# Three feed-forward units at the start of an encoder kernel loaded by blocks of rows, and transposes moved a tick later

## The chip, the cores and the metric

The kernel runs on one core of one Trainium2 chip. The metric is the device time of one execution in microseconds. The engines are TensorE (PE in the profile; its weight loads are PEld), VectorE (DVE), ScalarE (ACT), GpSimd (POOL) and SyncE (SP), which issues most of the loads.

## The reference, cut to what matters

A trunk of two layers over 256 tokens of width 1024. Each layer is a SwiGLU feed-forward, a mixer with three branches, and a second SwiGLU feed-forward:

```
for l in range(2):
    x = x + 0.5 * swiglu(rms_norm(x, g1), w1, w3, w2)         # w1, w3: 1024 x 2816, w2: 2816 x 1024
    h = rms_norm(x, gm);  z = h @ w_in                        # 1024 x 6752, cut into the three branches' inputs and the gates
    y_na  = neighborhood_attention(q, k, v, rpb)
    y_gla = rms_norm(gla_bidirectional(...)) * silu(gr)       # gated linear attention
    y_mla = mla_attention(...)
    x = x + sum_i(sigmoid(gate_i) * (y_i @ w_br_i)) @ w_out
    x = x + 0.5 * swiglu(rms_norm(x, g2), w1', w3', w2')
swiglu(h, w1, w3, w2) = (silu(h @ w1) * (h @ w3)) @ w2
```

All data are float32. Three products of split numbers (hi x hi, hi x lo, lo x hi) stand for one float32 product.

## The kernel before

Weights come in units of 1 MB (128 x 2048 float32) in the order of their use. SP loads a unit into a `raw` tile (three of them); ScalarE copies it to its high part (L142) and VectorE subtracts to get the low part (L148), two halves each, into an `hl` tile (four of them). TensorE multiplies high and low parts with those of the transposed activations `xT`. `unit()` sees to it that a unit and the first half of the next are split; `fill()` splits further ahead.

The order of all instructions is the order in which the Python code issues them; each engine executes its own list in that order. Side work (drains, norms, attention steps) is written as generators. `spawn(gen, wait)` puts one on a list; each `tick()`, called after a burst of matmuls, counts the waits down and runs a generator to its next `yield n`, which sets its wait to n ticks. `finish()` runs a generator to its end at once.

PSUM has eight banks: four with the tag `acc` for bursts (`acc_t`) and four with the tag `ta` for transposes and attention products (`tr_t`, `at_t`). Buffers of a tag go round, so a new tile waits until the last reader of the tile four back has finished.

The first feed-forward has no transposes of x: `start_first` loads x already transposed (`xT` in memory) and scales it by the norm's gain (`gcol`), since the row factor can be multiplied in later. It deals with the first two w1/w3 units: unit 0 by quarters of two k-steps each, interleaved with the loads of xT, unit 1 by halves. Each unit has 8 k-steps of 128 rows; w1 and w3 are the two halves b, and each k-step and half takes three matmuls of 256 columns (`part`). Then `fform` does the 20 other units, each with 16 matmuls of 512 columns (the high weights against high and low xT at once) and 16 of 256. `rs_bcast` (its two transposes are L298) broadcasts the row factors once they are known; in the first feed-forward this stands behind the third unit, and the drains of the units before it are started there. A drain (`fdrain`) reads the accumulators (L480 on ScalarE, L481 on VectorE; L485 and L486 for the first two units), multiplies by the row factor, applies silu (L487, L489) and splits the result (L491, L493).

The feed-forward's output (`wide_out`) keeps four banks, two for each half t of the tokens, over all eleven w2 units. In the mixer the linear attention's last steps are: add its parts to `gy` (L1092), squares and row factors (L1095, L573), eight products `gy * factor * silu(gr)` (L1103), then eight transposes of `gy` (L695, by `four`), split by L246 and L247. The transposed q of the neighbourhood attention comes from `na_tr` (also L695). The branches' products are multiplied with the gates (L1181, L1184), summed (L1186), transposed by `mix_task` (L1195) and go through w_out.

## Time and profile before

| | us |
|---|---|
| median of three timed runs | 1257.64 (1256.57 to 1257.86) |
| the profiled execution, its own time | 1256.21 |
| its span in the trace | 1254.4 |
| TensorE busy | 1237.7 |
| VectorE busy | 894.8 |
| ScalarE busy | 710.4 |
| GpSimd busy | 219.4 |

The page's parts are numbered: part 1 is the busy time of each engine, part 4 the chain of work that ended last, part 5 the costliest groups of instructions. Times in the trace count from the span's start. In a timeline a run of like instructions is one row: start, length from the first start to the last end, engine, line, operation, output and inputs, shape, count, and in brackets the idle time of the engine before it with what ended it. A row can be cut by the stretch that was asked for, and its times then still are those of the whole instructions in it.

### The profile page before, as it was taken

What the parts mean: (1) busy time and instruction counts of PE and PEld (TensorE: products, weight loads), DVE (VectorE), ACT (ScalarE), POOL (GpSimd) and SP (SyncE); (2) the same over time, 40 slices, a digit from 0 to 9 for tenths busy, and PEclk for the clock granted to TensorE, in tenths of its full rate; (3) what the DMA queues carried; (4) which work ended last, traced back from release to release, by engine and by line L of the source; (5) the groups of instructions that cost most, each with busy time, mean ns of one, the idle gap of its engine ahead of it and who ended that gap; (6) DMA issues with size and microseconds to landing.
All of it is one profiled execution on the core that took longest, in us unless ns stands there. A gap on an engine that the chain in (4) does not pass through costs nothing.

```text
span 1254.4 us, 18062 instructions
## 1 busy us (share of the span) xinstructions
PE 1237.7 (99%) x6996; PEld 1058.5 (84%) x6996; DVE 894.8 (71%) x1382; ACT 710.4 (57%) x1303; POOL 219.4 (17%) x167
## 2 busy tenths in 40 slices
PE   7999999999999999999999999999999999999998
PEld 7888888889987888888888888888899878888887
DVE  5888736679755868887378886375896577788862
ACT  6556535657665465655366555355686644665541
POOL 0222101132011112221012220021322020122200
PEclk9999999999999999999999999999999999999999
DMA  8655644562543544556345556347526434555560
GB/s 304 214 185 201 234 169 160 175 222 93 197 171 132 198 172 170 200 181 248 142 171 222 184 185 241 128 162 246 175 91 208 166 134 171 199 201 174 196 235 34
DMA packets 37942, 228.58 MB, mean 182 GB/s; under 512 B 5776, under 2 KB 6928, under 8 KB 13280
## 3 DMA queue, kind: packets, MB, share of 16 engines
q1 hardware_dynamic: 37680, 227.36, 51.1%
q8 instruction: 55, 0.90, 0.3%
q14 instruction: 31, 0.25, 0.1%
q0 software_dynamic: 32, 0.07, 0.0%
q10 hardware_dynamic: 144, 0.00, 0.0%
HBM read 224.26 MB, written 1.05 MB: 180 GB/s over the span
## 4 chain that ended last, share of the span: by engine, by line
PE 93%; DVE 4%; ACT 1%; DMA 1%; issue 1%; POOL 0%; DVEq 0%; SPq 0%; ACTq 0%
PE acc L372 86%; PE ta L372 4%; DVE hl L148 2%; PE ta L695 1%; DMA raw<-in_l_f_w 1%; PE ta L263 1%; ACT junk L1095 0%; POOL sm L573 0%; PE ta L782 0%; ACT hl L142 0%; PE ta L1195 0%; PE ta L680 0%; DVE s L489 0%; DVE s L1181 0%; DVE s L1103 0%
## 5 line engine op out<-in xcount | busy, mean ns | idle before, releaser
L148 DVE TENSOR_TENSOR hl<-raw,hl 128x1024 fp32r<-128x1024 f32 (+2 forms) x422 | 568.1, 1386 | 95.4 <-ACT hl L142 84.5
L142 ACT ACTIVATE hl<-raw 128x1024 fp32r<-128x1024 f32 (+2 forms) x422 | 417.1, 1040 | 103.8 <-PE acc L372 89.9
L372 PE MATMUL acc<-xT,hl 128*128 128x512 f32 (+1 forms) x2768 | 472.8, 332 | 0.9 <-DVE s L481 0.5
L372 PEld LDWEIGHTS acc<-xT,hl 128*128 128x128 f32 x2768 | 413.6, 188 | 57.8 <-DVE s L481 0.8
L372 PE MATMUL acc<-hl,xT 128*128 128x512 f32 (+1 forms) x1584 | 361.8, 383 | 0.0
L372 PEld LDWEIGHTS acc<-hl,xT 128*128 128x128 f32 x1584 | 291.8, 188 | 46.9 <-issue 1.7
L372 PE MATMUL acc<-hl,s 128*128 128x512 f32 x1344 | 312.3, 392 | 0.9 <-DVE s L481 0.9
L372 PEld LDWEIGHTS acc<-hl,s 128*128 128x128 f32 x1344 | 252.0, 189 | 54.2 <-DVE s L481 1.3
L482 POOL TENSOR_TENSOR s<-s,rsb 128x512 f32<-128x512 f32 x80 | 111.9, 1399 | 355.8 <-DVE s L481 355.8
L491 ACT ACTIVATE s<-s 128x256 fp32r<-128x256 f32 x82 | 34.2, 418 | 172.5 <-DVE s L489 172.5
L481 DVE TENSOR_TENSOR s<-acc,s 128x256 f32<-128x256 f32 x158 | 59.7, 419 | 58.5 <-ACT s L480 58.5
L573 POOL TENSOR_TENSOR sm<-sm,mhalf 128x4 f32<-128x4 f32 (+2 forms) x24 | 35.8, 1493 | 200.4 <-DVE sm L577 198.9
L284 POOL TENSOR_TENSOR sm<-sm,mhalf 128x1 f32<-128x1 f32 x12 | 14.1, 1176 | 295.1 <-DVE sm L283 295.1
L480 ACT ACTIVATE s<-acc 128x256 f32<-128x256 f32 x158 | 50.6, 371 | 0.0
L266 ACT ACTIVATE xT<-ta,gain 128x128 fp32r<-128x128 f32 x80 | 22.8, 368 | 35.6 <-PE ta L263 35.6
L247 DVE TENSOR_TENSOR s<-ta,s 128x512 fp32r<-128x512 f32 (+1 forms) x46 | 26.7, 604 | 22.6 <-ACT s L246 22.3
L246 ACT ACTIVATE s<-ta 128x512 fp32r<-128x512 f32 (+1 forms) x46 | 23.0, 531 | 34.4 <-PE ta L695 14.7
L487 ACT ACTIVATE s<-s 128x256 f32<-128x256 f32 x82 | 34.2, 419 | 11.2 <-POOL s L482 0.8
L550 DVE SCALAR_TENSOR_TENSOR x<-acc,x 128x512 f32<-128x512 f32 (+1 forms) x20 | 11.3, 580 | 39.7 <-PE acc L372 39.7
L372 PEld LDWEIGHTS ta<-s,s 64*64 64x64 f32 (+3 forms) x720 | 30.6, 145 | 7.0 <-issue 5.9
L372 PE MATMUL ta<-s,s 64*64 64x128 f32 (+4 forms) x720 | 35.9, 260 | 0.0
L493 DVE TENSOR_TENSOR s<-s,s 128x256 fp32r<-128x256 f32 x82 | 34.0, 416 | 1.9 <-ACT s L491 1.9
(161 smaller groups left out, 643.9 us busy)
## 6 DMA issues: line engine op xcount, KB each, us to landing
raw<-in_l_f_w SPq DMA_DIRECT2D x124, 1024.0 KB, 4.8
raw<-in_l_in_g SPq DMA_DIRECT2D x16, 816.0 KB, 4.4
raw<-in_l_in_late SPq DMA_DIRECT2D x8, 1024.0 KB, 4.9
raw<-in_l_out SPq DMA_DIRECT2D x8, 1024.0 KB, 4.8
raw<-in_l_f_up SPq DMA_DIRECT2D x6, 1024.0 KB, 4.8
raw<-in_l_in_m SPq DMA_DIRECT2D x4, 1024.0 KB, 4.7
raw<-in_l_in_gr SPq DMA_DIRECT2D x4, 1024.0 KB, 4.9
raw<-in_l_in_r SPq DMA_DIRECT2D x4, 1024.0 KB, 4.8
```

Of the source, the lines that this page charges most:

```text
L142: ACT.activation(out=hls[j][:, 0, sl], in_=raws[j][:, sl], func=AF.Copy)
L148: DVE.tensor_tensor(out=hl[:, 1, sl], in0=r[:, sl], in1=hl[:, 0, sl].bitcast(F32), op=ALU.subtract)
L246: ACT.activation(out=hi, in_=ps, func=AF.Copy)
L247: DVE.tensor_tensor(out=lo, in0=ps, in1=hi.bitcast(F32), op=ALU.subtract)
L372: PE.matmul(out=out, lhsT=lhsT, rhs=rhs, start=start, stop=stop, skip_group_check=True)
L480: ACT.activation(out=g[:, j, :], in_=a[j][:, 256:], func=AF.Copy)
L481: DVE.tensor_tensor(out=g[:, j, :], in0=a[j][:, :256], in1=g[:, j, :], op=ALU.add)
L482: POOL.tensor_tensor(out=g, in0=g, in1=rb[:, None, :].to_broadcast([128, 2, 256]), op=ALU.mult)
L487: ACT.activation(out=g[:, 0, :], in_=g[:, 0, :], func=AF.Silu)
L491: ACT.activation(out=o[:, 0, :], in_=g[:, 0, :], func=AF.Copy)
L493: DVE.tensor_tensor(out=o[:, 1, :], in0=g[:, 0, :], in1=o[:, 0, :].bitcast(F32), op=ALU.subtract)
L573: POOL.tensor_tensor(out=r[:, :n], in0=ss[:, :n], in1=mhalf[:, :n], op=ALU.pow)
```

## The change

- The first three w1/w3 units, not two, go through `start_first` (FIRST_R = 3). They and xT are loaded by blocks of rows: k-step 0, k-step 1, then pairs of k-steps; for each block first xT, then that block of each of the three units (128 x 256 for one k-step, 128 x 512 for two). They land in tiles of the scratch pool (`s2`), not in `raw`.
- For each block the three units are split and multiplied one after the other. Each unit has one bank (tag `ta`), w1 in its first half and w3 in its second.
- Ahead of them TensorE does eight matmuls of 512 columns on a tile of zeros (bfloat16), which VectorE clears first.
- gcol's load is issued before ScalarE's first activation; the identity is loaded by SP behind the fourth unit, no more by POOL; x comes behind it, then the fifth and sixth units.
- `rs_bcast` stands behind the fourth unit; it is followed by that unit's drain and then those of the first three. No unit is held back any more.
- In every feed-forward `wide_out` takes the two banks of t = 1 from `ta` instead of `acc`. The mixer's `wide_out` keeps `acc`.
- In the mixer three kinds of transposes come one tick later: those of `gy` (`yield 2`), of q (`spawn(..., 4)`) and of the merged branches (`spawn(mix_task, 3)`).

```diff
-FIRST_R = 2
+FIRST_R = 3
+WARM = 8
         def start_first():
+            zero = junk(512)
+            DVE.memset(zero, 0.0)
+            ps = tr_t()
+            for _ in range(WARM):
+                PE.matmul(out=ps, lhsT=zero[:, :128], rhs=zero, start=True, stop=True, skip_group_check=True)
             POOL.memset(mhalf, -0.5)
             POOL.memset(ones, 1.0)
-            ACT.activation(out=junk(1), in_=ones, func=AF.Copy)
             nc.scalar.dma_start(out=gcol, in_=T["gcol"])
-            nc.gpsimd.dma_start(out=idt, in_=T["ident"])
-            xr = [s2((128, 2, 256)) for _ in range(4)]
...
-            for q in range(4):
-                sl = slice(q * 512, q * 512 + 512)
-                nc.sync.dma_start(out=xr[q], in_=T["xT"][:, 2 * q:2 * q + 2, :])
-                nc.sync.dma_start(out=raws[0][:, sl], in_=units[0][0][:, sl])
...
+            xr = [s2() for _ in range(4)]
+            rw = [[s2() for _ in range(4)] for _ in range(FIRST_R)]
+            groups = ((0, 1), (1, 2), (2, 4), (4, 6), (6, 8))
+            at = lambda tiles, a, b: tiles[a // 2][:, a % 2 * 256:a % 2 * 256 + (b - a) * 256]
+            for a, b in groups:
+                nc.sync.dma_start(out=at(xr, a, b), in_=T["xT"][:, a:b, :])
+                for j in range(FIRST_R):
+                    nc.sync.dma_start(out=at(rw[j], a, b), in_=units[j][0][:, a * 256:b * 256])
+            ACT.activation(out=small(1), in_=ones, func=AF.Copy)
...
+            dma_to(FIRST_R)
+            nc.sync.dma_start(out=idt, in_=T["ident"])
             for t in range(2):
                 nc.sync.dma_start(out=x[:, t, :], in_=T["x"][t * 128:(t + 1) * 128, :])
...
+            dma_to(FIRST_R + 2)
+
+            def part(acc, hl, k):
+
+                for c in range(2):
+                    o = acc[:, c * 256:c * 256 + 256].rearrange("p (t n) -> p t n", t=2)
+                    a = k * 256 + c * 128
+                    mm(o, hl[:, 0, a:a + 128], xT[:, :, 0, k, :], k == 0 and c == 0, False)
                     mm(o, hl[:, 0, a:a + 128], xT[:, :, 1, k, :], False, False)
                     mm(o, hl[:, 1, a:a + 128], xT[:, :, 0, k, :], False, k == 7)
 
-            accs = [[at_t(), at_t()], [acc_t(), acc_t()]]
...
+            accs = [at_t() for _ in range(FIRST_R)]
+            for a, b in groups:
+                sl = slice(a * 256, b * 256)
+                for k in range(a, b):
...
+                for j in range(FIRST_R):
+                    ACT.activation(out=hls[j][:, 0, sl], in_=at(rw[j], a, b), func=AF.Copy)
+                    DVE.tensor_tensor(out=hls[j][:, 1, sl], in0=at(rw[j], a, b), in1=hls[j][:, 0, sl].bitcast(F32),
+                                      op=ALU.subtract)
+                    for k in range(a, b):
+                        part(accs[j], hls[j], k)
+            st["next"] = FIRST_R
+            split_to(2 * FIRST_R + 2)
...
-        def wide_out(first, lhs, nu, done):
+        def wide_out(bank1, lhs, nu, done):
...
-                        accs[t] = (acc_t(), acc_t())
+                        accs[t] = (bank1(), bank1()) if t else (acc_t(), acc_t())
...
                 if i == (FIRST_R if first is not None else 2):
                     rs_bcast()
-                    if first is not None:
-                        for j in range(2):
-                            drains[j] = run(fdrain(j, first[j][0][:, :256], first[j][1][:, :256]))
-                        for j, a in held:
-                            drains[j] = run(fdrain(j, a))
-                if "x" in rs_b:
-                    drains[i] = run(fdrain(i, acc))
-                else:
-                    held.append((i, acc))
+                drains[i] = run(fdrain(i, acc))
+                if first is not None and i == FIRST_R:
+                    for j in range(FIRST_R):
+                        drains[j] = run(fdrain(j, first[j][:, :256], first[j][:, 256:]))
                 tick()
...
-            wide_out(True, lhs, NCH, done)
+            wide_out(at_t, lhs, NCH, done)
...
-                yield 1
+                yield 2
                 for j in range(2):
                     ps = four(gy, j * 256)
...
-            q_tk = spawn(na_tr("q", nq), 3)
+            q_tk = spawn(na_tr("q", nq), 4)
...
-                            mt[h, t] = spawn(mix_task(h, t), 2)
+                            mt[h, t] = spawn(mix_task(h, t), 3)
...
-            wide_out(True, lhs, 4, done)
+            wide_out(acc_t, lhs, 4, done)
```

On SP's queue, at the program's start, before (`in_xT` is the transposed x, `in_l_f_w` the w1/w3 units, `s_90` to `s_93` the four tiles for xT):

```order
L313 DMA s_90<-in_xT 128x512
L314 DMA raw<-in_l_f_w 128x512
L313 DMA s_91<-in_xT 128x512
L314 DMA raw<-in_l_f_w 128x512
L313 DMA s_92<-in_xT 128x512
L314 DMA raw<-in_l_f_w 128x512
L313 DMA s_93<-in_xT 128x512
L314 DMA raw<-in_l_f_w 128x512
L317 DMA raw<-in_l_f_w 128x1024 x2
L128 DMA raw<-in_l_f_w 128x2048
L323 DMA x<-in_x 128x1024 x2
```

And now, the first ten loads and those behind the last block (`s_98` to `s_101` hold xT, `s_102` to `s_113` the blocks of the three units):

```order
L317 DMA s_98<-in_xT 128x256
L319 DMA s_102<-in_l_f_w 128x256
L319 DMA s_106<-in_l_f_w 128x256
L319 DMA s_110<-in_l_f_w 128x256
...
L317 DMA s_99<-in_xT 128x512
L319 DMA s_103<-in_l_f_w 128x512
...
L319 DMA s_113<-in_l_f_w 128x512
L129 DMA raw<-in_l_f_w 128x2048
L326 DMA idt<-in_ident 128x128
L328 DMA x<-in_x 128x1024 x2
L129 DMA raw<-in_l_f_w 128x2048 x6
```

Twenty loads of blocks now stand ahead of the first whole unit; x and the identity stand behind it.

On VectorE, around the products of `gy` in layer 0's mixer, before (`hl` are the splits of weights, `gates` the products of the second branch with its gates, `s_3848` and `s_3857` the low halves of the transposed `gy`):

```order
L1181 TENSOR_TENSOR s_3810<-acc,gates 128x512
L148 TENSOR_TENSOR hl<-raw,hl 128x1024 x2
L1103 SCALAR_TENSOR_TENSOR s_3691<-s_3691,sm,s_1928 128x128 x4
L1103 SCALAR_TENSOR_TENSOR s_3702<-s_3702,sm,s_1955 128x128 x4
L1184 TENSOR_TENSOR gates<-acc,gates 128x512
L247 TENSOR_TENSOR s_3848<-ta,s_3847 128x512
L247 TENSOR_TENSOR s_3857<-ta,s_3856 128x512
```

And now (`s_3920` and `s_3929` are these low halves):

```order
L1177 TENSOR_TENSOR s_3863<-acc,gates 128x512
L149 TENSOR_TENSOR hl<-raw,hl 128x1024 x2
L1099 SCALAR_TENSOR_TENSOR s_3744<-s_3744,sm,s_1981 128x128 x4
L1099 SCALAR_TENSOR_TENSOR s_3755<-s_3755,sm,s_2008 128x128 x4
L1180 TENSOR_TENSOR gates<-acc,gates 128x512 x2
L149 TENSOR_TENSOR hl<-raw,hl 128x1024 x2
L248 TENSOR_TENSOR s_3920<-ta,s_3919 128x512
L248 TENSOR_TENSOR s_3929<-ta,s_3928 128x512
```

The low halves of the transposed `gy` now stand behind one more gate product and one more pair of splits.

On TensorE, where layer 0's mixer passes from its branches to w_out, before (`s_3857` is the low half of the transposed `gy`, the inputs of L1195 are the merged rows, `xT` their transposed form):

```order
L372 MATMUL acc<-hl,s_3857 128x512
L1195 MATMUL ta<-idt,s_3792 128x128 x4
L372 MATMUL acc<-hl,xT 128x512 x12
L1195 MATMUL ta<-idt,s_3810 128x128 x4
L372 MATMUL acc<-hl,xT 128x512 x60
```

And now (`s_3929` is the low half of the transposed `gy`):

```order
L373 MATMUL acc<-hl,s_3929 128x512
L1191 MATMUL ta<-idt,s_3770 128x128 x4
L373 MATMUL acc<-hl,xT 128x512 x12
L1191 MATMUL ta<-idt,s_3845 128x128 x4
L373 MATMUL acc<-hl,xT 128x512 x12
L1191 MATMUL ta<-idt,s_3863 128x128 x4
L373 MATMUL acc<-hl,xT 128x512 x48
```

Each of the four groups of transposes stands one burst of twelve matmuls later, so two of them, not one, stand behind the first burst of w_out.

## Rows read from the trace of the kernel before

**Rows 1.** Page, parts 1 and 4: busy time by engine; the chain by engine.
```profile
PE 1237.7 (99%) x6996; PEld 1058.5 (84%) x6996; DVE 894.8 (71%) x1382; ACT 710.4 (57%) x1303; POOL 219.4 (17%) x167
...
PE 93%; DVE 4%; ACT 1%; DMA 1%; issue 1%; POOL 0%; DVEq 0%; SPq 0%; ACTq 0%
```

**Rows 2.** What TensorE waited for: us in total, times, longest us.
```profile
PE ta L372 <- ACT hl L341: 6.2, 1, 6.2
PE ta L695 <- DVE s L1103: 4.2, 4, 1.6
PE acc L372 <- DVE s L481: 1.4, 2, 0.9
...
PE ta L1195 <- DVE s L1186: 0.4, 2, 0.2
PE ta L695 <- DVE s L830: 0.2, 1, 0.2
```

**Rows 3.** Timeline of the start: start, length, engine, line, operation.
```profile
4.67 0.91 ACT L339 ACTIVATE xT<-s,gcol 128x256 fp32r<-128x256 f32 x2 [2.45 <-DMA gcol<-in_gcol]
...
5.49 0.61 ACT L341 ACTIVATE hl<-raw 128x512 fp32r<-128x512 f32 x1
...
7.68 0.62 ACT L341 ACTIVATE hl<-raw 128x512 fp32r<-128x512 f32 x1
...
8.94 0.88 DVE L343 SCALAR_TENSOR_TENSOR xT<-s,gcol,xT 128x256 fp32r<-128x256 f32 x2
...
9.73 0.69 DVE L347 TENSOR_TENSOR hl<-raw,hl 128x512 fp32r<-128x512 f32 x1
...
12.10 0.62 ACT L341 ACTIVATE hl<-raw 128x512 fp32r<-128x512 f32 x1
...
26.88 0.38 PE L298 MATMUL ta<-idt,sm 128*128 128x128 f32 x2
```

**Rows 4.** Timeline of TensorE alone, three stretches of the start.
```profile
6.88 3.36 PE L372 MATMUL ta<-xT,hl 128*128 128x256 f32 x14
...
15.61 5.66 PE L372 MATMUL acc<-xT,hl 128*128 128x256 f32 x45 [0.41 <-DVE hl L148]
...
21.11 5.93 PE L372 MATMUL acc<-xT,hl 128*128 128x256 f32 x33
```

**Rows 5.** Windows of the start: engines' busy us (instructions), PEclk, DMA share, GB/s.
```profile
2.00:6.00 4.00, 0.00 (x0) 0.00 (x0) 0.79 (x2) 1.54 (x5) 0.02 (x1) 1.00 0.84 223
6.00:11.00 5.00, 4.85 (x24) 4.63 (x25) 3.76 (x8) 2.88 (x7) 0.00 (x0) 1.00 1.01 374
```

**Rows 6.** Page, part 5: count | busy us, mean ns | idle before.
```profile
L372 PE MATMUL acc<-hl,s 128*128 128x512 f32 x1344 | 312.3, 392 | 0.9 <-DVE s L481 0.9
...
L491 ACT ACTIVATE s<-s 128x256 fp32r<-128x256 f32 x82 | 34.2, 418 | 172.5 <-DVE s L489 172.5
```

**Rows 7.** Timeline: the first feed-forward's two waits for accumulators.
```profile
44.69 35.48 PE L372 MATMUL acc<-xT,hl 128*128 128x512 f32 x199 [0.48 <-DVE s L481]
...
139.06 2.19 PE L372 MATMUL acc<-hl,s 128*128 128x512 f32 x8 [0.91 <-DVE s L481]
```

**Rows 8.** Timeline around the transposes of gy in layer 0.
```profile
398.32 2.35 DVE L148 TENSOR_TENSOR hl<-raw,hl 128x1024 fp32r<-128x1024 f32 x2
400.59 2.18 DVE L1103 SCALAR_TENSOR_TENSOR s<-s,sm,s 128x128 f32<-128x128 f32 x8
...
401.07 0.50 PE L695 MATMUL ta<-idt,s 128*128 128x128 f32 x2 [1.63 <-DVE s L1103]
...
402.03 1.26 PE L695 MATMUL ta<-idt,s 128*128 128x128 f32 x6 [0.46 <-DVE s L1103]
...
403.29 1.36 DVE L247 TENSOR_TENSOR s<-ta,s 128x512 fp32r<-128x512 f32 x2
```

**Rows 9.** Windows behind the transposes of gy: layer 0, then layer 1.
```profile
402.81:406.21 3.40, 3.40 (x11) 2.72 (x10) 1.84 (x3) 2.93 (x4) 1.29 (x1) 0.50 0.58 243
...
1023.10:1026.50 3.40, 3.40 (x17) 2.81 (x17) 2.02 (x4) 2.73 (x4) 1.30 (x1) 1.00 0.56 231
```

More of the change, by code (lines that the diff above doesn't have):

```diff
@@ L308, in start_first @@
-            xr = [s2((128, 2, 256)) for _ in range(4)]
-            for j in range(2):
-                raws[j] = wp.tile([128, 2048], F32, name="raw", tag="raw", bufs=RAW_BUFS)
-            for q in range(4):
-                sl = slice(q * 512, q * 512 + 512)
-                nc.sync.dma_start(out=xr[q], in_=T["xT"][:, 2 * q:2 * q + 2, :])
-                nc.sync.dma_start(out=raws[0][:, sl], in_=units[0][0][:, sl])
-            for p in range(2):
-                sl = slice(p * 1024, p * 1024 + 1024)
-                nc.sync.dma_start(out=raws[1][:, sl], in_=units[1][0][:, sl])
@@ L334, in start_first @@
-            raw0 = raws[0]
-            for q in range(4):
-                sl = slice(q * 512, q * 512 + 512)
-                ks = (2 * q, 2 * q + 1)
-                for k in ks:
-                    ACT.activation(out=xT[:, :, 0, k, :], in_=xr[q][:, k % 2, :].rearrange("p (t n) -> p t n", t=2),
+            accs = [at_t() for _ in range(FIRST_R)]
+            for a, b in groups:
+                sl = slice(a * 256, b * 256)
+                for k in range(a, b):
+                    ACT.activation(out=xT[:, :, 0, k, :], in_=at(xr, k, k + 1).rearrange("p (t n) -> p t n", t=2),
@@ L345, in start_first @@
                                              scalar=gcol[:, k:k + 1], in1=xT[:, :, 0, k, :].bitcast(F32),
                                              op0=ALU.mult, op1=ALU.subtract)
-                DVE.tensor_tensor(out=hl[:, 1, sl], in0=raw0[:, sl], in1=hl[:, 0, sl].bitcast(F32), op=ALU.subtract)
-                for b in range(2):
-                    part(accs[0], hl, ks, b)
-            st["next"] = 2
-            for p in range(2):
-                split_to(3 + p)
-                for b in range(2):
-                    part(accs[1], hls[1], range(4 * p, 4 * p + 4), b)
-                if p == 0:
-                    split_to(4)
@@ L357, in start_first @@
-            split_to(6)
+                for j in range(FIRST_R):
+                    ACT.activation(out=hls[j][:, 0, sl], in_=at(rw[j], a, b), func=AF.Copy)
+                    DVE.tensor_tensor(out=hls[j][:, 1, sl], in0=at(rw[j], a, b), in1=hls[j][:, 0, sl].bitcast(F32),
+                                      op=ALU.subtract)
+                    for k in range(a, b):
+                        part(accs[j], hls[j], k)
+            st["next"] = FIRST_R
+            split_to(2 * FIRST_R + 2)
             for t in range(2):
@@ L496, in fform @@
                 hl = unit()
-                acc = [(at_t() if first is not None and i == 3 else acc_t()) for _ in range(2)]
+                acc = [acc_t() for _ in range(2)]
                 for b in range(2):
@@ L508, in fform @@
                     rs_bcast()
-                    if first is not None:
-                        for j in range(2):
-                            drains[j] = run(fdrain(j, first[j][0][:, :256], first[j][1][:, :256]))
-                        for j, a in held:
-                            drains[j] = run(fdrain(j, a))
-                if "x" in rs_b:
-                    drains[i] = run(fdrain(i, acc))
-                else:
-                    held.append((i, acc))
+                drains[i] = run(fdrain(i, acc))
+                if first is not None and i == FIRST_R:
+                    for j in range(FIRST_R):
+                        drains[j] = run(fdrain(j, first[j][:, :256], first[j][:, 256:]))
                 tick()
-            us, drains, held = {}, {}, []
+            us, drains = {}, {}
             if first is None:
@@ L531, in ffn @@
                 utr = spawn(tr_task(us), 2)
-            for i in range(2, NB):
+            for i in range(2 if first is None else FIRST_R, NB):
                 fform(i)
```

16 lines of the change are left out of this document (4 added, 12 removed).

## The prediction

> **What bounds the kernel now.** Part 1 and part 4 of the page come first: TensorE is busy for 1237.7 of 1254.4 us and makes up 93% of the chain that ended last [rows 1]. So only what TensorE waits for, or does at half speed, can be won back. Next the list of TensorE's waits, longest first [rows 2]: 6.2 us before the first matmul; 4.2 us in four waits for the products of L1103 (two in each layer's mixer); 1.4 us in two waits for an accumulator that L481 still reads; 0.4 and 0.2 us at two kinds of transposes. That is about 12 us. Time lost at half speed stands in no list of waits. It is seen where the same matmul takes twice as long: in the first microseconds 14 matmuls of 256 columns fill 3.36 us, later 45 fill 5.66 us [rows 4], and in 402.81 to 406.21 the granted clock is 0.50, the lower of the two levels, 1.2 GHz [rows 9].
>
> A busy row is no proof of full pace, so I take the pace from rows with a count. A row runs from its first start to its last end, and matmuls overlap: with about 0.29 us for the last one, (5.66 - 0.29) / 44 = 0.122 us from start to start. At the beginning (3.36 - 0.34) / 13 = 0.23 us. The ordinary w1/w3 unit: (5.93 - 0.29) / 33 x 32 matmuls = 5.5 us, I use 5.6 [rows 4].
>
> **The change part by part.**
>
> *Start.* Before, two units go through the special start; the third is an ordinary one, and the transposes of L298 behind it mark its end, 26.88 [rows 3]. After, three units go block by block: 3 x 48 = 144 matmuls of 256 columns, at 0.122 us 17.6 us. The columns are the same in number as before (48 x 256 against 16 x 512 + 16 x 256 in the third unit, 5.9 against 5.6 us, so 0.3 us dearer). So the question is when they begin, at what clock, and whether the blocks arrive.
>
> Begin: ScalarE starts on xT at 4.67, when gcol lands; it then does two k-steps of xT (0.91) and a quarter of a unit (0.61) before TensorE can start at 6.15 [rows 2, 3]. After, it does one k-step (0.46) and a 128x256 copy (nearest row 0.42 [rows 6]): 4.67 + 0.88 = 5.55. gcol is now issued ahead of the table load, which may give some tenths; I leave them for the range.
>
> Clock: the eight matmuls on zeros depend only on a memset, so they fill the time in which TensorE now idles. Before, matmuls ran at half pace for about the first four microseconds after TensorE began. I take it that the zeros pay for this and that the real matmuls run at 0.122 us from the first.
>
> Feed: for two k-steps of three units ScalarE needs 0.91 + 3 x 0.61 = 2.7 us, VectorE 0.88 + 3 x 0.69 = 3.0 us [rows 3], TensorE 36 x 0.122 = 4.4 us. Both keep ahead. Loads: the start before had landed 1 MB by 7.68 (the second quarter of the first unit is copied then) and 2 MB by 12.10 (the last quarter) [rows 3]. After, the third unit's k1 block completes the first MB and is wanted at 5.55 + 2.2 + 1.5 = 9.2; its k2-k3 block completes the second MB, copied from 12.1, ready 12.7, wanted at 5.55 + 4.4 + 2.9 = 12.8. So the loads just suffice. I add 0.2 us for small waits: the three units end at 5.55 + 17.6 + 0.2 = 23.3, against 26.88: **3.6 us**. Bounds: below, blocks of 1 KB a row cost no more per byte and gcol comes 0.4 us earlier (4.2 us won); above, see the rivals. The splits of the third unit now stand in the start too; the margins just given hold them. On SP's queue 20 loads stand ahead of the fourth unit's, before it was 11 and the x rows; the identity moves there from POOL. Identity and x are wanted only by the squares and transposes that come one unit later than before.
>
> What is late next: after the fourth unit the drains of four units stand on VectorE, with the splits of units 5 and 6. Before, this gave the wait of 0.48 us at 44.69 [rows 7]. I keep that wait as it is: the raw units come when they did, so VectorE gains no time there.
>
> *Bank of the FFN's output.* In the first FFN TensorE waits 0.91 us at 139.06 for L481, which drains the last unit from the accumulators that t = 1 wants [rows 7]. With t = 1 in the other four banks no drain stands in front: **0.9 us**, in one FFN of four; the others show no such wait [rows 2].
>
> *Transposes of gy.* VectorE does a pair of splits (398.32, 2.35 us) and then the eight products (400.59 to 402.77); TensorE has nothing else queued and waits 1.63 + 0.46 us [rows 8]. One tick later means twelve more matmuls of 512 columns first: 12 x 312.3/1344 = 2.8 us [rows 6]. TensorE then arrives at 401.07 - 1.63 + 2.8 = 402.2, with the last products due 402.77 and needed last. So 2.1 us goes in each layer, **4.2 us** in all [rows 2]. What is late next: the low halves of gy's transposes (1.36 us for two [rows 8]) must be ready when the third branch begins, 24 matmuls (5.6 us) behind the transposes' end, 408.8. VectorE has before that two gate products (a 128x512 operation, 0.69 each [rows 3]) and a pair of splits (2.35): 402.8 + 1.4 + 2.35 + 1.36 = 407.9. It holds by 0.9 us.
>
> *Clock behind that wait.* In layer 0 the wait of 2.1 us is followed by 3.4 us at 0.50; in layer 1 the same wait is followed by full clock [rows 9]. Without the wait I expect no fall: 3.4 us x one half = **1.7 us**.
>
> *Mixed transposes and q transposes.* Each waits 0.2 us (0.4 and 0.2 in all [rows 2]); a tick of 2.8 us covers that: **0.6 us**. The first output matmul of t = 0 follows its transposes by 12 matmuls instead of 24; the split (0.6 on ScalarE, 0.69 on VectorE) fits into 2.8 us unless a pair of splits goes first, which the order on VectorE does not show.
>
> Sum: 3.6 + 0.9 + 4.2 + 1.7 + 0.6 = 11.0 us. The profiled execution took 1256.2 us (span 1254.4 and 1.8 around it), which is 1.4 below the median of the runs shown; 1256.2 - 11.0 = **1245.2 us**.
>
> **The rivals.**
>
> *A. The zeros do not lift the clock.* They end about a microsecond before real work begins, and in layer 0 the clock fell behind waits of only 1.63 and 0.46 us, while it did not in layer 1 [rows 8, 9]. If the first real matmuls ran at 0.23 us until about 10.3, as before, some 21 instead of 39 would be done by then: 18 x 0.122 = 2.2 us lost, 1247.4. The Trainium skill (TensorE: Matmul & The Clock Gate, "What's actually happening") says that half rate is the resting state and that the hardware's look at activity is not tied to the kernel's start. By that rule the point at which the clock rises may move from run to run; with a rise before 5.5 us the sum stays, with a later one it is this rival. This trace cannot show it: it has one start.
>
> *B. Small blocks starve TensorE.* Between 2 and 6 us the loads move 223 GB/s, between 6 and 11 374 GB/s [rows 5]. A 256 KB piece at 223 GB/s takes 1.2 us. If a 128 KB block took as long, the four blocks of k1 would end 4.8 us behind the first four (5.5), at 10.3, with the copy 10.7, and be wanted at 9.2: 1.5 us lost. If the twelve 256 KB blocks stayed at that pace as well, the last would come at 10.3 + 14.1 = 24.4, ready at 25.0, and be wanted at 21.6: 3.4 us lost, 1248.6. For it: rows of 1 KB instead of 2 KB. Against it: the early rate is also that of queues just starting. The Trainium skill (DMA: Bandwidth & Descriptors, "Measured (HBM→SBUF, 128 partitions, SWDGE, issued from GpSimd)") gives 138 GB/s for 64 KB and 341 for 1 MB and asks for 1 MB pieces. At its 64 KB rate the first MB would take 7.6 us, an estimate, and come about 1 us late, 1246.2; the 374 GB/s here came with 256 KB pieces, more than its table gives them.
>
> *C. The wait moves to the third branch.* The margin of 0.9 us there is smaller than one pair of splits. If a pair goes first, 2.35 - 0.9 = 1.4 us in each layer, and the clock falls once: 1245.2 + 2.9 + 1.7 = 1249.8.
>
> *D. Slower.* With t = 1 in the transposes' banks, each FFN before the last one holds two of four such banks to its end, and the next norm's transposes may have to wait for VectorE's last additions behind a pair of splits: 2.35 + 0.69, and 1.7 for a clock that falls after each, 4.7 x 3 = 14.2 us: 1259.4. It outweighs the gain from 11.0 / 3 = 3.7 us a block. Against it: those transposes read what the same additions write, so they wait for them in any case.
>
> **How the numbers follow.** Forecast 0.62, A 0.14, B 0.10, C 0.08, D 0.04, no change for a reason not seen 0.02. Range: below, 4.2 for the start, the 0.48 gone and up to 2 us more where TensorE refills after each of the waits removed: about 1242; above, A to C: 1249. Of the first three cases little is left outside 1241.5 to 1249. What a measurement here can tell from no change is 0.2%, 2.5 us: faster 0.94 (forecast, A, B, C), same 0.02, slower 0.04.
>
> **What would show it.** First real matmul near 5.5 and 0.12 us spacing from it on (against A); no gap over 0.5 us among the first 144 (against B); the broadcast transposes, now behind the fourth unit, near 29; no wait of TensorE for the products of gy nor, at the FFN's output, for an accumulator; granted clock 1.00 in the gates' stage; no wait at the third branch's first matmuls (against C). The forecast is wrong if the three units end after 25 us, or if a half-clock stretch stands in another place.

## The result, and the profile after

The change took the kernel from 1256.31 us (median of 6 runs, 1254.61 to 1257.86) to **1247.45 us** (6 runs, 1246.18 to 1247.79): ratio 0.9928, 95% interval 0.9915 to 0.9941. The forecast was 1245.2 us, the range 1241.5 to 1249.0. Where 11.0 us were expected, 8.9 came. That 1247.45 is also the time of the prediction's rival A (1247.4) is chance: the terms that make it up are others, as shown below. The profiled execution took 1247.79 us, with a span of 1246.0.

TensorE's busy time and the engines' shares stand as they stood [rows 1]. The list of waits (us in total, times, longest us) is another one:

```profile
PE acc L373 <- DVE xT L248: 2.2, 4, 0.8
PE ta L308 <- DVE junk L305: 1.2, 1, 1.2
PE ta L373 <- ACT hl L352: 0.8, 2, 0.6
PE ta L373 <- DVE hl L353: 0.4, 2, 0.2
```

Against [rows 2]: the 4.2 us for the products of gy, the 1.4 us for accumulators and the 0.6 us at the q and mixed transposes are gone. New are 2.2 us for xT, in four waits, and 1.2 us in four small waits inside the start (L352, L353). The 1.2 us on L308 are the time before the matmuls on zeros; before the change 6.2 us stood there, before the first matmul of all.

The start on TensorE, where [rows 3, 4] had 6.88 for the first 14 matmuls shown and 26.88 for the end of the third unit:

```profile
1.17 3.60 PE L308 MATMUL ta<-junk 128*128 128x512 bf16 x8 [1.17 <-DVE junk L305]
4.26 5.24 PE L373 MATMUL ta<-xT,hl 128*128 128x256 f32 x36
10.08 0.50 PE L373 MATMUL ta<-xT,hl 128*128 128x256 f32 x2 [0.59 <-ACT hl L352]
10.81 2.90 PE L373 MATMUL ta<-xT,hl 128*128 128x256 f32 x22 [0.23 <-DVE hl L353]
13.93 0.51 PE L373 MATMUL ta<-xT,hl 128*128 128x256 f32 x2 [0.21 <-ACT hl L352]
14.65 10.18 PE L373 MATMUL ta<-xT,hl 128*128 128x256 f32 x82 [0.22 <-DVE hl L353]
24.67 6.18 PE L373 MATMUL acc<-xT,hl 128*128 128x512 f32 x32
30.69 0.38 PE L299 MATMUL ta<-idt,sm 128*128 128x128 f32 x2
30.82 19.55 PE L373 MATMUL acc<-xT,hl 128*128 128x512 f32 x109
```

Real work begins at 4.26, 1.3 us earlier than forecast. Four times TensorE stops in the middle, and the three units end at 24.67 instead of 23.3. This start is not the same in every execution: in five other traces of it the three units end at 24.12, 24.13, 24.63, 24.74 (without zeros) and 26.39. The last row shows one thing more: 109 matmuls run on past 45 us, where [rows 7] had the wait of 0.48.

The same stretch as windows (busy us by engine, granted clock, DMA share, GB/s), against 374 GB/s in 6 to 11 us in [rows 5]:

```profile
2.00:6.00 4.00, 4.00 (x16) 2.48 (x15) 1.88 (x5) 3.05 (x8) 0.00 (x0) 1.00 0.80 240
6.00:10.00 4.00, 3.50 (x30) 3.29 (x28) 2.22 (x6) 2.27 (x6) 0.00 (x0) 1.00 0.90 279
10.00:14.00 4.00, 3.48 (x25) 3.07 (x25) 1.45 (x4) 1.33 (x4) 0.00 (x0) 1.00 0.96 281
```

From 6 us on the loads are slower than before, though the column of DMA share says that the engines are hardly idle. SyncE's own queue shows a part of the reason (start, length, count of issues):

```profile
0.72 0.38 SPq L317 DMA_DIRECT2D s<-in_xT  x1
1.16 1.37 SPq L319 DMA_DIRECT2D s<-in_l_f_w  x3
2.57 0.43 SPq L317 DMA_DIRECT2D s<-in_xT  x1
3.05 1.38 SPq L319 DMA_DIRECT2D s<-in_l_f_w  x3
```

An issue every 0.47 us (eight of them from 0.72 to 4.43): with 128 KB each that is 131072 B / 0.47 us = 279 GB/s at most, a ceiling over the first window's 240. That the second window moved 279 as well is chance: the loads that land in it are mostly blocks of 256 KB, issued at the same 0.47 us. What the small issues in front do is that these blocks are issued late: the four loads of the second megabyte were issued at 4.47 to 5.89, in the kernel before at 2.58 to 4.43.

In the gates' stage of layer 0 TensorE now has, where [rows 8] had two waits:

```profile
397.90 1.13 PE L691 MATMUL ta<-idt,s 128*128 128x128 f32 x8
398.79 13.89 PE L373 MATMUL acc<-hl,s 128*128 128x512 f32 x60
...
417.62 2.11 PE L373 MATMUL acc<-hl,xT 128*128 128x512 f32 x8 [0.35 <-DVE xT L248]
...
421.88 2.12 PE L373 MATMUL acc<-hl,xT 128*128 128x512 f32 x8 [0.78 <-DVE xT L248]
```

No wait for gy, and full pace behind it: 13.89 us for 60 matmuls, and the granted clock of the window, which was 0.50 in [rows 9], is 1.00:

```profile
398.90:402.30 3.40, 3.40 (x16) 2.80 (x16) 3.40 (x4) 3.40 (x5) 2.97 (x2) 1.00 0.53 219
```

But at the output product TensorE waits for the low half of xT. VectorE in the same stretch:

```profile
399.77 4.18 DVE L149 TENSOR_TENSOR hl<-raw,hl 128x1024 fp32r<-128x1024 f32 x2
...
406.27 4.23 DVE L149 TENSOR_TENSOR hl<-raw,hl 128x1024 fp32r<-128x1024 f32 x2
...
413.21 2.35 DVE L149 TENSOR_TENSOR hl<-raw,hl 128x1024 fp32r<-128x1024 f32 x2
...
416.88 0.68 DVE L248 TENSOR_TENSOR xT<-ta,xT 128x512 fp32r<-128x512 f32 x1
```

Two pairs of splits take 4.2 us where the third takes 2.35, and no idle time stands ahead of any of them: VectorE is late. GpSimd at the same time:

```profile
399.33 3.54 POOL L1182 TENSOR_TENSOR s<-s,gates 128x512 f32<-128x512 f32 x2 [5.15 <-DVE gates L1180]
405.89 3.53 POOL L1182 TENSOR_TENSOR s<-s,gates 128x512 f32<-128x512 f32 x2 [3.02 <-DVE gates L1180]
```

The two long pairs lie beside the second branch's four additions on GpSimd. In the kernel before, the additions of the same stage stood further apart:

```profile
403.44 1.29 POOL L1186 TENSOR_TENSOR s<-s,gates 128x512 f32<-128x512 f32 x1 [5.15 <-DVE gates L1184]
408.11 3.45 DVE L148 TENSOR_TENSOR hl<-raw,hl 128x1024 fp32r<-128x1024 f32 x2
408.33 2.14 POOL L1186 TENSOR_TENSOR s<-s,gates 128x512 f32<-128x512 f32 x1 [3.60 <-DVE gates L1184]
```

An addition beside no split takes 1.29 us, and a pair of splits beside one addition 3.45 (a second such pair, at 413.56, 3.44). With the later transposes of gy two gate products, and so two additions, fall together with each of two pairs: 4.18 + 4.23 against 3.45 + 3.44, 1.5 us more of VectorE's time in each layer. (The run below that takes this edit back has 3.45 and 3.44 again.)

### The profile page after: what moved, and what is told of

The parts are those of the page before. It is cut to its first block, busy times and chain, and to the rows that moved or that the text cites. A ratio compares the mean times of both kernels' runs of the same rounds, so it can differ in the third digit from the quotient of the medians.

```text
span 1246.0 us, 18152 instructions
## 1 busy us (share of the span) xinstructions
PE 1237.4 (99%) x7020; PEld 1058.4 (85%) x7020; DVE 895.5 (72%) x1390; ACT 710.2 (57%) x1308; POOL 217.6 (17%) x165
## 4 chain that ended last, share of the span: by engine, by line
PE 92%; DVE 5%; DMA 1%; issue 1%; ACT 1%; SPq 0%; DVEq 0%; ACTq 0%
PE acc L373 75%; PE ta L373 14%; DVE hl L149 3%; PE ta L691 1%; DMA raw<-in_l_f_w 1%; PE ta L264 1%; DMA s<-in_xT 1%; ACT junk L1091 0%; DVE gates L1180 0%; DVE s L1180 0%; PE ta L778 0%; DVE s L1182 0%; SPq L319 0%; DVE s L1099 0%; PE ta L676 0%
## 5 line engine op out<-in xcount | busy, mean ns | idle before, releaser
L149 DVE TENSOR_TENSOR hl<-raw,hl 128x1024 fp32r<-128x1024 f32 (+1 forms) x418 | 565.3, 1393 | 95.3 <-ACT hl L143 84.9
L143 ACT ACTIVATE hl<-raw 128x1024 fp32r<-128x1024 f32 (+1 forms) x418 | 412.6, 1040 | 108.2 <-PE ta L373 87.3
L373 PE MATMUL acc<-xT,hl 128*128 128x256 f32 (+1 forms) x2720 | 466.9, 333 | 0.1
L373 PEld LDWEIGHTS acc<-xT,hl 128*128 128x128 f32 x2720 | 407.9, 188 | 56.7 <-DVE hl L149 0.4
L373 PE MATMUL acc<-hl,s 128*128 128x512 f32 x816 | 194.4, 391 | 0.0
L373 PEld LDWEIGHTS acc<-hl,s 128*128 128x128 f32 x816 | 152.4, 188 | 32.2 <-issue 0.7
L373 PE MATMUL ta<-hl,s 128*128 128x512 f32 (+1 forms) x624 | 148.0, 386 | 0.0
L373 PEld LDWEIGHTS ta<-hl,s 128*128 128x128 f32 x624 | 116.2, 188 | 22.5
```

The costliest lines, as they stand in the source:

```text
L143: ACT.activation(out=hls[j][:, 0, sl], in_=raws[j][:, sl], func=AF.Copy)
L149: DVE.tensor_tensor(out=hl[:, 1, sl], in0=r[:, sl], in1=hl[:, 0, sl].bitcast(F32), op=ALU.subtract)
L373: PE.matmul(out=out, lhsT=lhsT, rhs=rhs, start=start, stop=stop, skip_group_check=True)
```

## The experiments

Beside these runs the kernel before took 1256.15 to 1256.34 us (medians), so times are compared directly with 1247.45. Differences under about 1 us between medians are not clear of the spread of single executions (1.6 us in the changed kernel). A trace shows one execution each; where its start differs from that of the changed kernel's trace, the text says so.

**Mixed transposes a tick earlier, as before.**

```
-                            mt[h, t] = spawn(mix_task(h, t), 3)
+                            mt[h, t] = spawn(mix_task(h, t), 2)
```

> The merged rows' transposes again wait two ticks, all else as in the changed kernel. Theory: the four new waits of TensorE for the low halves of xT (2.2 us idle in all, about 2.5 with the refill) come from this edit alone, so they go and the old two waits of 0.2 us come back: the changed kernel less about 2 us, 1245.4. Rival: the waits come from VectorE being behind since TensorE no longer stands still for gy, whatever the transposes' place: the waits stay or move, within 0.5 us of the changed kernel.

Measured: 1248.60 us (1248.07 to 1249.54), ratio 0.9938 (0.9926 to 0.995). The theory that this edit had done harm fell; the rival had the waits right, and its 0.5 us too small. The waits:

```profile
PE ta L1191 <- DVE s L1182: 4.1, 2, 2.1
```

A wait that was 0.4 us in all before the change [rows 2] is now 4.1. With TensorE no longer held at gy, VectorE is that much further behind. The edit is worth 1.2 us, since the later tick takes the transposes out of VectorE's lag; what is left of the lag shows as 2.2 us at the output.

**Transposes of gy a tick earlier, as before.**

```
-                yield 2
+                yield 1
                 for j in range(2):
                     ps = four(gy, j * 256)
```

> The transposes of gy again come one tick earlier, all else as in the changed kernel. Theory: the two waits of 2.1 us come back, and in some runs a stretch of half clock behind one of them: 4.2 to 5.9 us slower than the changed kernel, 1251.7 to 1253.4, less up to 2.2 if the later waits at the output shrink because VectorE catches up. Rival: the waits were paid for elsewhere anyway, under 2 us.

Measured: 1250.23 us (1249.31 to 1251.21), ratio 0.995 (0.9938 to 0.9962). The wait list has the old row again, and none for xT:

```profile
PE ta L691 <- DVE s L1099: 4.2, 4, 1.6
```

and behind the wait in layer 0 the clock fell (windows: PEclk 0.51):

```profile
397.20:400.60 3.40, 3.40 (x12) 2.85 (x12) 2.53 (x6) 2.56 (x4) 1.29 (x1) 0.51 0.71 294
```

So the edit does take away 4.2 us of waits and 1.7 us of half clock, and is worth 2.8 us net: 2.2 us of the gain is given back at the output. In the traces the missing 0.9 us is the start, which went better in this one: the broadcast transposes stand at 29.78 where the changed kernel's trace has them at 30.69.

**No matmuls on zeros.**

```
-WARM = 8
+WARM = 0
```

> The eight matmuls on zeros are left out, all else as in the changed kernel. Theory (the start is bound by its loads): TensorE then runs at half pace for some four microseconds from 4.3, has done the first two k-steps at about 10.4 instead of 9.3, still before the block of the third unit that lands at 13.2; the three units end within 0.3 us of 24.7: no change in the time. Rival (the clock is what the start lives on): the 17 matmuls more at half pace cost 1.6 to 2 us, 1249.3.

Measured: 1247.45 us (1245.62 to 1248.47), ratio 0.9927 (0.9915 to 0.9939): no difference. The trace's record of the granted clock begins with its rise to full, here at 9.78 us. The first 38 matmuls ran without a stop, up to 11.71, and the three units ended at 24.74 (24.67 with zeros).

**Blocks of the three units laid out one behind the other in memory.**

```
-                    nc.sync.dma_start(out=at(rw[j], a, b), in_=units[j][0][:, a * 256:b * 256])
+                    nc.sync.dma_start(out=at(rw[j], a, b), in_=T[f"blk{j}_{a}"])
...
```

> The blocks of the first three units are stored packed in memory, each block's 128 rows one behind the other, so that a load reads one closed region and not pieces of 1 or 2 KB from rows 8 KB apart; number, size and order of the loads are the same. Theory (the spacing in memory is what slows the loads): between 6 and 14 us the rate rises from about 280 GB/s toward the 374 to 430 of the kernel before, 2 MB land before 12 instead of at 13.2, the three units end near 23 instead of 24.7, 1.5 us gained at most: 1246.0. Rival (pieces of 1 and 2 KB and twenty loads are slow by themselves): no change in the rate nor in the time.

Measured: 1247.10 us (1246.92 to 1249.08), ratio 0.9928 (0.9916 to 0.994): no clear difference. Windows:

```profile
2.00:6.00 4.00, 4.00 (x17) 2.15 (x16) 1.55 (x4) 2.60 (x8) 0.00 (x0) 1.00 0.83 236
6.00:10.00 4.00, 3.30 (x28) 3.10 (x26) 2.02 (x6) 2.00 (x6) 0.00 (x0) 1.00 0.80 266
10.00:14.00 4.00, 3.16 (x24) 2.96 (x25) 3.96 (x9) 3.88 (x9) 0.00 (x0) 1.00 1.05 398
```

Layout alone matters from 10 us on: 398 GB/s, where the changed kernel has 281 and five other traces of its start 289 to 333. In the first 10 us, where TensorE starves, it changes nothing: something else holds the rate there. The three units end at 24.16, no earlier than in two of those traces (24.12 and 24.13).

**Additions of the second branch on VectorE.**

```
-                            e = DVE if i == 2 else POOL
-                            e.tensor_tensor(out=m, in0=m, in1=g, op=ALU.add)
+                            DVE.tensor_tensor(out=m, in0=m, in1=g, op=ALU.add)
```

> In the second branch of the mixer the four additions to the mixed sum are done by VectorE instead of GpSimd; the rest is the changed kernel. Theory (VectorE is what TensorE waits for at the mixer's output product, and GpSimd's additions make it later: a pair of VectorE splits takes 4.2 us beside them and 2.35 us elsewhere, twice per layer): VectorE gives up 4 x 0.69 = 2.8 us per layer to the additions and gets back 2 x 1.85 = 3.7 us, so it is 0.9 us earlier per layer; the waits of TensorE for xT at the output product fall from 2.2 us in all to about 0.4, the pairs of splits all take about 2.35 us, and the time falls by 1.0 to 1.8 us, to 1245.6 to 1246.4 us. Rival (the splits are long for another reason, or the additions' place in VectorE's order delays the splits of the third branch): the pairs stay at 4.2 us or the waits move to the third branch, and the time rises by up to 2 x 2.8 = 5.5 us, to 1247.5 to 1253 us.

Measured: 1246.30 us (1244.84 to 1246.81), ratio 0.9917 (0.9904 to 0.9929). More work on the late engine made it earlier:

```profile
400.67 0.69 DVE L1181 TENSOR_TENSOR s<-s,gates 128x512 f32<-128x512 f32 x1
...
402.61 2.35 DVE L149 TENSOR_TENSOR hl<-raw,hl 128x1024 fp32r<-128x1024 f32 x2
...
408.73 2.35 DVE L149 TENSOR_TENSOR hl<-raw,hl 128x1024 fp32r<-128x1024 f32 x2
```

Every pair in this stage is back at 2.35 us, and TensorE's waits for xT fell from 2.2 us to 0.7. That GpSimd's additions lengthen VectorE's splits, and that these set most of the output's wait, is shown. The 1.2 us understate the edit, by this trace: its start went worse (broadcast transposes at 32.04 against 30.69), and at the last mixed transposes of layer 1 it was still ahead (1039.92 against 1040.89), which makes 2.3 us.

**The old start with all other edits.** Here the lines differ from the kernel before.

```
-            wide_out(True, lhs, NCH, done)
+            wide_out(at_t, lhs, NCH, done)
...
-                yield 1
+                yield 2
...
-            q_tk = spawn(na_tr("q", nq), 3)
+            q_tk = spawn(na_tr("q", nq), 4)
...
-                            mt[h, t] = spawn(mix_task(h, t), 2)
+                            mt[h, t] = spawn(mix_task(h, t), 3)
```

> The kernel before with all edits of the change but the start: banks of the FFN's output, gy transposes, q transposes and mixed transposes as in the changed kernel. Theory (the start is worth 2.3 to 2.8 us, read from the broadcast transposes, 30.7 us after the change and in its repeats down to 29.8, against about 32.6 before, and the 0.48 us wait behind them): 1249.8 to 1250.3 us. Rival 1 (the predicted 3.6 us or more are there and lost elsewhere): 1251 us or more. Rival 2 (the start gives nothing that lasts to the end): 1247.5 us.

Measured: 1249.69 us (1249.35 to 1251.16), ratio 0.9948 (0.9937 to 0.996). The new start is worth 2.2 us, as the timelines said. Here the fourth unit ends at 32.70 and the accumulator's wait is there, against 30.82 and none after the change (1.9 + 0.5 = 2.4):

```profile
32.70 11.46 PE L372 MATMUL acc<-xT,hl 128*128 128x512 f32 x64
44.65 1.56 PE L372 MATMUL acc<-xT,hl 128*128 128x512 f32 x7 [0.49 <-DVE s L481]
```

**Half as many issues for the first two row blocks: sixteen loads of 256 KB, two for each row block, each in one piece of memory.**

```
-            for a, b in groups:
-                nc.sync.dma_start(out=at(xr, a, b), in_=T["xT"][:, a:b, :])
-                for j in range(FIRST_R):
-                    nc.sync.dma_start(out=at(rw[j], a, b), in_=units[j][0][:, a * 256:b * 256])
...
+            for k in range(8):
+                for p in range(2):
+                    nc.sync.dma_start(out=pk[k][p], in_=T["first"][2 * k + p])
...
```

> The start's xT and first three units laid out in memory as sixteen 256 KB pieces, two for each of the eight row blocks (xT beside unit 0, unit 1 beside unit 2), each a load of its own: the first two row blocks need 4 DMA issues instead of 8, the copies and matmuls go one row block at a time, in the same order. Theory (the early loads are held by SyncE's issuing, 0.47 us for each, so that 128 KB pieces come at 279 GB/s, which is the measured 279 to 281 GB/s): all row blocks land at about 2 MB by 10 us (13.2 in the changed kernel), no wait over 0.5 us among the first 144 matmuls, the three units end at 22.5 to 23.3 us instead of 24.67 (4.3 + 144 x 0.12 = 21.6 is the bound by TensorE), and the time falls by 1.0 to 1.8 us to 1245.6 to 1246.4 us. Rival (the chip's memory or the DMA engines give no more than 240 to 280 GB/s this early): the landings of the first 1 MB stay at 7 us or later, the wait near 9 us stays, and the time is 1247.1 us as with the packed blocks.

A row block's first load holds xT and unit 0, its second units 1 and 2. Measured: 1245.46 us (1245.18 to 1245.95), ratio 0.9913 (0.99 to 0.9925): 2.0 us better than the change. Windows:

```profile
2.00:6.00 4.00, 4.00 (x13) 2.17 (x12) 1.73 (x5) 2.86 (x9) 0.00 (x0) 1.00 0.99 326
6.00:10.00 4.00, 4.00 (x31) 4.00 (x31) 3.35 (x10) 3.40 (x11) 0.00 (x0) 1.00 1.02 370
```

and TensorE, without one stop among the 144:

```profile
4.54 18.75 PE L369 MATMUL ta<-xT,hl 128*128 128x256 f32 x144
23.12 5.81 PE L369 MATMUL acc<-xT,hl 128*128 128x512 f32 x32
28.77 0.38 PE L299 MATMUL ta<-idt,sm 128*128 128x128 f32 x2
```

326 GB/s in the window that had 240 with small blocks cut out of larger rows (the change) and 236 with the units' small blocks in one piece each. This run changes the number of issues and, for xT too, the layout; it does not say which decided. Large pieces alone do not do it either: the old start issues 256 KB pieces, cut out of larger rows, and moved 223 in this window [rows 5], 215 in the run above (64 KB of the identity came beside them). Small packed pieces and large strided ones are both slow, large packed ones fast. The rows of 2 KB instead of 1 KB are a small part: a packet of 1 KB took 46 ns in the traces and one of 2 KB 84 (medians), so 1 KB costs a tenth more per byte, while the rate rose by more than a third.

**Two queues: the third unit's first two blocks issued by ScalarE.**

```
-                    nc.sync.dma_start(out=at(rw[j], a, b), in_=units[j][0][:, a * 256:b * 256])
+                    e = nc.scalar if j == 2 and b <= 2 else nc.sync
+                    e.dma_start(out=at(rw[j], a, b), in_=units[j][0][:, a * 256:b * 256])
```

> The changed kernel, but the third unit's first two blocks are issued by ScalarE's queue instead of SyncE's; sizes, layout and order of use are the same. Theory (SyncE's issuing at 0.47 us each holds the early loads): the six issues left on SyncE end at 3.5 us instead of 4.4, every later block is issued 0.9 us earlier, the wait near 9 us is 0.5 to 0.9 us shorter and the three units end 0.5 to 0.9 us earlier than 24.67; time 1246.6 to 1247.0 us, hardly to be told from 1247.4, so the landings decide. Rival (the DMA engines hold it): the second and third row blocks land when they did (5.1 to 7.2 us, 8.6 us and later), and the time is 1247.4 us; ScalarE's first copy is up to 0.3 us later.

Measured: 1246.72 us (1246.24 to 1246.96), ratio 0.9922 (0.9909 to 0.9934): 0.7 us better, not clear of the spread. Same sizes, same layout, and the window of 2 to 6 us rose to 272 GB/s, where the changed kernel has 240 and five other traces of its start 238 to 245. The window of 6 to 10 us did not rise (267). The three units end 0.8 us earlier than in the changed kernel's trace, 0.2 us earlier than in the best of the others, and of the stops two of 0.2 us are left (the second at 13.91):

```profile
2.00:6.00 4.00, 3.93 (x16) 2.11 (x15) 1.52 (x4) 3.39 (x8) 0.00 (x0) 1.00 0.87 272
```

```profile
10.19 3.49 PE L374 MATMUL ta<-xT,hl 128*128 128x256 f32 x24 [0.22 <-DVE hl L354]
...
23.91 5.81 PE L374 MATMUL acc<-xT,hl 128*128 128x512 f32 x32
```

The Trainium skill (DMA: Bandwidth & Descriptors, "Rules for kernel authors") says that spreading loads over queues gives no bandwidth and only saves issue time. The runs agree in part: issue time, 0.47 us a load, was a part of what held the first window, where a second queue gave some 30 GB/s more; it did not cure the start.

**Paired loads and the additions on VectorE.** The edits of those two experiments together.

> The start of the paired loads and the additions on VectorE together. Theory (the two gains lie 370 us apart and nothing between them is shared, so they add): three units end near 23.1 us, waits of TensorE for xT at the output product fall from 2.2 to 0.7 us; 1245.5 less 1.5 gives 1244.0 us, 1243.5 to 1244.5. Rival (the additions gained by other means, or the earlier start only moves a wait): 1245.0 to 1245.5 us.

Measured: **1242.59 us** (1241.22 to 1242.83), ratio 0.9884 (0.9867 to 0.99), 4.9 us under the change and the fastest version run. Besides the 1.2 us before the zeros, TensorE waits in the list only for xT:

```profile
PE acc L369 <- DVE xT L248: 0.7, 2, 0.4
```

The sum of the two gains, 2.0 + 1.2, is 3.2, and the expectation's 1243.5 was still too high. The traces show where the rest lies. TensorE is 0.8 us ahead of the paired loads at the broadcast transposes, where its clock rose earlier (4.29 us against 7.14):

```profile
28.00 0.38 PE L299 MATMUL ta<-idt,sm 128*128 128x128 f32 x2
```

At the last mixed transposes of layer 1 it is 3.35 us ahead (1035.84 against 1039.19). So the additions are worth 2.3 to 2.6 us in the traces, as above, and 2.0 + 0.8 + 2.3 = 5.1 comes near the 4.9.

**Paired loads without zeros.** WARM = 0 once more.

> The kernel with the paired loads, without the eight matmuls on zeros. Theory (the zeros were worth nothing only because the loads held the start; now that they no longer do, the clock counts): the clock is granted at 9.8 us as in the run without zeros instead of 7.14, the 2.7 us between are worth half, the three units end about 1.3 us later than 23.12, time 1246.3 to 1246.9 us. Rival (loads still set the end of the three units, or the clock comes no later): three units end by 23.4 us, 1245.5 us.

Measured: 1246.97 us (1246.2 to 1247.41), ratio 0.9921 (0.9907 to 0.9934): 1.5 us slower than with zeros. Where loads no longer hold TensorE, the clock does. The pace is read from the counts of matmuls in a window, which take in those that only reach into it. The column of the granted clock is no help here: it reads 1.00 until the trace's record of the clock begins, with the rise to full clock, at 8.97 us without zeros. Without zeros:

```profile
7.00:9.00 2.00, 2.00 (x11) 2.00 (x11) 1.81 (x6) 2.00 (x7) 0.00 (x0) 1.00 1.05 397
```

and with zeros, in the fastest version:

```profile
7.00:9.00 2.00, 2.00 (x19) 2.00 (x18) 1.96 (x6) 1.99 (x7) 0.00 (x0) 1.00 1.00 365
```

11 matmuls in 2 us is half pace, 19 full; the three units end at 23.92 without zeros, at 23.12 and 22.35 in the two traces with them. Against the first of these that is 0.8 us, and 0.7 in the times of the two profiled executions (1246.65 and 1245.95).

**Banks of the FFN's output as before.**

```
-            wide_out(at_t, lhs, NCH, done)
+            wide_out(acc_t, lhs, NCH, done)
```

> The changed kernel with the banks of the FFN's output product as before. Theory (the wait of 0.91 us near 139 us and 0.5 us in the third FFN that the row of before showed): TensorE's waits for the accumulator come back with 0.5 to 1.4 us in all, 1248.0 to 1248.8 us. Rival (with the other edits this wait is gone anyway): no such wait, 1247.4 us.

Measured: 1248.17 us (1247.76 to 1249.71), ratio 0.9932 (0.9918 to 0.9946). The wait is back, once and at half its size; the 0.5 us that the expectation puts into another FFN were the start's wait of 0.48, which did not return:

```profile
PE acc L373 <- DVE s L482: 0.4, 1, 0.4
```

## Why the prediction was right, and where it was off

**What bounds the kernel.** Right: every gain here, and every one added since, is a wait or half-clock time of TensorE. It counted the waits that stood in the list; the new 2.2 us came from an engine that this list did not show as late.

**Start: 3.6 us forecast, 2.2 measured.** The mechanism was right, the size of two terms was not. *Begin*: forecast 5.55, came at 4.26, because ScalarE could start on xT at 3.40 (4.67 in [rows 3]): 1.3 us better than the sum. gcol was issued 0.2 us earlier (0.72 instead of 0.91) and was under way for 2.7 us instead of 3.7; why, no run separates. *Feed*: "the loads just suffice" failed. It took the landings of before (1 MB by 7.68, 2 MB by 12.10) for loads that need twice as many issues for the first megabyte. That megabyte was in time (7.22); the second, issued behind it, was not. The third unit's k2-k3 block was copied at 13.24, not 12.1 (it landed between 12.03 and 12.88 in five other traces of this start), and the waits and late blocks ate the early begin and 1.4 us more (24.67 against 23.3). The fourth unit then took 6.18 us where it took 5.81 behind the paired loads. *The 0.48 wait kept*: it went, 0.5 us in favour. So 2.2 us is a sum of misses in both directions, not a forecast met.

**Clock in the start.** "The zeros pay for this" holds only in part: the record of the clock has the rise at 5.63 us, 1.4 us behind the first real matmul, which so did not run at 0.122 us. In this kernel the zeros are worth nothing: with them TensorE runs ahead of the loads and waits, without them it is at half pace until 9.78, stops once for 0.22 us, and ends the three units at 24.74, inside the range of the traces with zeros. With the paired loads they are worth 1.5 us by the medians.

**Bank: 0.9 forecast, 0.7 measured** by taking it back alone, a difference not clear of the spread. In that run's trace TensorE loses 0.85 us between the broadcast transposes (30.28, 30.69 in the changed kernel) and the first transposes of x (187.56, 187.12).

**Transposes of gy: 4.2 + 1.7 forecast, 2.8 net.** Both terms are seen to the digit in the run that takes the edit back. The margin at the third branch held, barely: the first low half of gy is ready at 404.55 and the first matmul that reads it starts at 404.80. What the argument missed is the price of a pair of splits, 2.35 us in its sum and 4.2 in the run, and what follows one stage further. VectorE had used TensorE's 2.1 us of standing still to catch up; without it, and with 1.5 us more in each layer for the splits beside the additions, VectorE is still behind when the output product wants xT.

**Mixed transposes and q transposes: 0.6 forecast.** The sentence that failed is the last of that step: the split "fits into 2.8 us unless a pair of splits goes first, which the order on VectorE does not show". A pair does go first (413.21 ahead of 416.88), and VectorE gets there late. So 2.2 us of waits stand where 0.4 stood. Yet the edit is not the cause: without it the wait is 4.1 us. Given the lag, it is worth 1.2 us, three times its forecast of 0.4. The q part was not tried alone.

Together, from the two profiled executions: 1.9 (fourth unit's end) + 0.5 + 0.9 + 4.2 + 1.7 + 0.6 - 2.2 = 7.6 of 1256.2 - 1247.8 = 8.4 us; 0.8 us is not placed. Taken back one at a time from the full change, the parts are worth 2.2 + 0.7 + 2.8 + 1.2 = 6.9 of 8.9; parts that share one lag do not add.

**The rivals.** *A*: the clock rose late, as it feared, but behind the loads that cost nothing. What it drew from the Trainium skill (TensorE: Matmul & The Clock Gate, "What's actually happening"), that the moment of the rise may move from run to run, is borne out: with the same zeros it came at 5.63 us after the change, at 7.14 with the paired loads and at 4.29 in the fastest version. *B* named the right place: this feed did starve TensorE. It priced the bytes of a block (1.2 us for 256 KB) and the row length; the issues behind one another and the layout are what the runs show, together and not separated. The blocks of k1 came by 7.22, not 10.3, and cost no wait; those behind them did. *C* had the right mechanism, a wait that moves to where VectorE is late, at the wrong place and without the clock's fall: 2.2 instead of 4.6 us. *D*: no such wait appeared.

**What would show it.** Right were: no waits for gy or the accumulator, no half clock in the gates' stage, no wait at the third branch. Wrong were: the first matmul near 5.5 (4.26), 0.12 us spacing from it on (only from 5.63), broadcast transposes near 29 (30.69) and no gap over 0.5 us (one of 0.59). Of the signs that would refute it neither came in this trace. Both came in the trace of the run with the additions on VectorE, whose start is the same: the three units ended at 26.39, and a stretch of half clock stood in the start. So how the start ends differs from one execution to the next.

## What to carry to other kernels

Read the issuing queue before cutting a load into blocks: bytes per issue over the time of an issue is a ceiling on the early rate, and what stands behind many small pieces is issued late. It is not the only limit: here large pieces had to lie packed in memory as well. When a wait of the busiest engine is taken away, list what the others did during it: an engine that used it to catch up will be late at the next meeting, so follow its queue one stage past the margin. A cheap operation moved to an idle engine is not free if it slows a neighbour's long ones.

## What the runs showed of the hardware

- An addition of 128x512 from SBUF took 0.69 us on VectorE and 1.29 us on GpSimd beside no split (403.44 in the kernel before); beside splits two took 3.54. Beside two of these on GpSimd, two VectorE splits (two SBUF inputs each) took 4.2 us instead of 2.35, beside one 3.45. The Trainium skill (GPSIMD Engine Reference, "1. Specifications") says that GpSimd shares its SBUF interfaces with VectorE and contends with instructions of two SBUF inputs; the traces agree, and give the price: 1.85 us of VectorE per pair of additions.
- SyncE issued a load every 0.47 us, 128 or 256 KB alike. Blocks of 256 KB in one piece of memory moved at 398 GB/s in 10 to 14 us, as rows of 2 KB cut out of larger ones at 281 (up to 333 in other traces). Such rows moved at 374 between 6 and 11 us in the kernel before [rows 5], so the stride alone does not set the rate; what does is open.
- The same start differs from trace to trace by more than a microsecond. In the run with the additions on VectorE one load landed late (the first unit's k2-k3 block at 10.66, against 9.31), TensorE waited 1.75 us, and the clock was then granted at 0.50 for 3.4 us:

```profile
12.70:16.10 3.40, 3.40 (x19) 3.40 (x18) 3.23 (x7) 3.08 (x7) 0.00 (x0) 0.50 1.04 400
```

The three units of that run ended at 26.39, and it was faster than the change all the same.
